# Computing v of all heads first, in 512-column matmuls over eight PSUM banks, and regrouping the projections around it

## The chip, the cores and the metric

The kernel runs on one core of a Trainium2 chip. The metric is the device time of one execution in microseconds, median of three runs. The core has a matrix engine (TensorE, PE in the profile), a vector engine (VectorE, DVE), an activation engine (ScalarE, ACT), GpSimd (POOL), SyncE (SP, which here issues most of the DMAs), and 16 DMA engines. Instructions of one engine are executed in the order in which they are queued; engines wait for each other by semaphores.

## The reference

One layer of a bidirectional encoder over 512 positions and 2048 features, all in float32:

```python
h = _rmsnorm(x, attn_norm_w[l])
proj = jnp.einsum('bsd,de->bse', h, w_in[l])
q_pre, fz_f, fz_b, i_pre, gate, b_gate, c_gate, h_conv = jnp.split(proj, SPLIT_OFFSETS, axis=-1)
y_rec = _hgrn2_mixer(q_pre, fz_f, fz_b, i_pre, gate, lbs_f[l], lbs_b[l], hgrn_norm_w[l])
y_conv = _short_conv_mixer(b_gate, c_gate, h_conv, conv_w[l])
mixed = jnp.concatenate([y_rec, y_conv], axis=-1)
x = x + jnp.einsum('bse,ed->bsd', mixed, w_out[l])
h2 = _rmsnorm(x, ffn_norm_w[l])
g, u = jnp.split(jnp.einsum('bsd,df->bsf', h2, w_gate_up[l]), 2, axis=-1)
x = x + jnp.einsum('bsf,fd->bsd', jax.nn.silu(g) * u, w_down[l])
return _rmsnorm(x, final_norm_w)
```

Each of the eight pieces of `proj` has 1024 features, which is 8 heads (or 8 convolution groups) of 128. `i_pre` is v of the recurrence, unchanged; q goes through silu; the forward and backward f give decays and keys. `_hgrn2_mixer` runs, for each head, a gated linear recurrence over the positions in both directions and a norm over the head's 128 features.

## The kernel before

**Arithmetic.** Every float32 operand is split into two parts of a faster format, hi (a cast on ACT, L143 or L959) and lo = x - hi (a subtraction on DVE, L133). A product of two such operands is three matmuls, hi x hi, hi x lo, lo x hi: `mm3`, L185 to L187. `gemm` makes one row block of a projection (128 features x 512 positions) from 16 blocks of 128 input features: 48 matmuls of 512 columns.

**Units.** Two row blocks of the projection that share the input are also computed as a `Unit` of seven products (a 2 x 2 scheme of Strassen's kind). The operand combinations of the activations, the "forms", are made once in `start`: `b11`, `b12`, `b21`, `b22` and the derived `t1` to `t4`. A product is 16 matmuls, eight of 512 columns (L1027) and eight of 256 (L1029). Sums and splits of the weights for each product are made on DVE and ACT just ahead of it, and DVE adds up the results.

**Stages around the change.**
- `start` loads the input x block by block (`kt`, 16 blocks), splits it, and computes v of head pairs 0 and 1 while the blocks arrive: for each block 8 outputs of 128 positions x 256 features, one `mm3` each, in eight banks. Then it makes three projections of head 0 (q, f forward, f backward) by `gemm`. The norm factor of the input is made inside the first two: `rstd_steps` sums the squares by small matmuls (L213), copies the sums and takes mean + eps on DVE (L218, L221), the power -1/2 on POOL (L224), multiplies it into a diagonal on DVE (L230), and spreads it over the partitions by a matmul (L235). The result is `R` (as a row) and `rk` (as a column).
- `stream` runs 15 units: q of heads 1 to 4, then convolution and gate rows. Two generators are stepped between products: `rest`, with what `start` left to do, and `later`, with silu and convolution steps. Results go to DRAM (`qd`, `gd`, `md`, `zd`, `vd`).
- `heads` runs the recurrence of the eight heads, one after the other. The recurrence of a head is nine dependent levels, each a few small matmuls (L262, L273, L280, L288, L316) with several DVE operations between, and a norm (L213 to L235 again). So that TensorE has work meanwhile, projections of later heads are put between: `windows` lists for each period what is computed in it, `size` counts it in segments of one `mm3`, and the recurrence's 15 steps are spread evenly over the segments (`PARTS`, `segment`). In these windows lie v of pairs 2 and 3 (`values_mm`, with 256-column matmuls, 384 in all), q of heads 5 to 7, f of heads 1 to 7, and convolution rows.
- `out_proj` and `ffn` follow.

The order on TensorE, DVE and ACT is the order in which the program is written (`manual_schedule`) in `start`, `stream`, `heads` up to its first yield, and `ffn`; later in `heads` that of TensorE alone.

Of the kernel before, what the change touches and what calls it, by code (L numbers as in the profile page):

```python
# [358 lines left out]
def start(k, xT, wi, wp, vd, zd):  # L359
# [9 lines left out]
    order = [j + 4 * i for i in (0, 2, 1, 3) for j in range(4)]  # L369

    def forms(j, xa, xb):
# [10 lines left out]
        for i, (name, src) in enumerate((("t1", b11), ("t2", b22), ("t4", b21))):  # L382
            f = k.slot(F32R, k.sp if 3 * j + i < 5 else k.hp)
            nc.scalar.copy(f[:, :H], src)
            F[name, j] = f[:, :H], f[:, H:], vap(f, 0, [[H, 2], [1, H]])
            todo.append((f[:, H:], src, f[:, :H].bitcast(F32)))
# [16 lines left out]
    for n, kt in enumerate(order):
# [8 lines left out]
        if kt % 2 == 0:  # L412
            j = kt // 2
            s = slice((j % 4) * T, (j % 4 + 1) * T)
            e = slice((j % 2) * T, (j % 2 + 1) * T)
            for i in range(2):
                nc.sync.dma_start(out=raw[i][j // 4][:, s], in_=wi[i, j // 4, :, s])
        if kt % 4 == 0:
            w = [[k.wp.tile([P, QW], F32R, tag=t, name=k.nm(t), bufs=HLB) for t in ("hi", "lo")]
                 for _ in range(2)]  # L420
# [21 lines left out]
    ws = k.weights(wp[0])  # L442
    held = []
    for i in range(2):
        for t in range(4):
            if t % 2 == 0:
                v = k.slot()
            h = v[:, (t % 2) * 256:(t % 2 + 1) * 256]
            if t % 2:
                nc.vector.tensor_copy(out=h, in_=pss[i][t][:, :256])  # L450
            else:
                nc.scalar.copy(h, pss[i][t][:, :256])
            held.append(h)
    act = [(kt, hT[kt]) for kt in range(KT)]
    rs = k.rstd_steps(k.ssum, DM, keep=k.xsum)

    def t3(j, x):
        h, l = [a[:, H:].bitcast(F32) for a in hT[j + 8][:2]]
        nc.vector.scalar_tensor_tensor(out=x, in0=x, scalar=col(C_ATT + j), in1=h,
                                       op0=ALU.mult, op1=ALU.subtract)  # L460
        k.sub(x, l, x)

    def rows():
        rc, pb = next(rs)
        nc.scalar.copy(k.R, pb)
        nc.vector.tensor_copy(out=k.rk, in_=rc)
        for n, h in enumerate(held):
            nc.scalar.activation(h, h, AF.Copy, scale=k.rk[:, n % 4:n % 4 + 1])
            nc.sync.dma_start(out=vd[n], in_=h)
# [8 lines left out]
    for i in range(3):
        ticks = [lambda: work(WORK2)] * KT
        if i == 0:  # L480
            ticks[10] = lambda: next(rs)
        if i == 1:
            ticks[2] = rows
            ticks[5] = lambda: store(0)
        if i < 2:
            ticks[3] = lambda: ws.extend(k.weights(wp[i + 1]))
        else:
            b12 = load_b12(k, xT)
            ticks[2] = lambda: store(1)
            for j in range(8):  # L490
                ticks[8 + j] = lambda j=j: t3(j, b12[j])
        zs.append(k.gemm([ws.pop(0) for _ in range(2)], act, tick=lambda: ticks.pop(0)()))
    for j in range(8):
        for name, kt, c in (("b11", j, lo), ("b21", j + 8, lo), ("b22", j + 8, hi), ("t3", j, hi)):
            F[name, j] = *[a[:, c] for a in hT[kt][:2]], hT[kt][2][:, :, c]

    def rest():
        while later:
# [4 lines left out]
        for j in range(8):
            h, l, _ = F["t3", j]
            nc.scalar.copy(h, b12[j])
            k.sub(l, b12[j], h.bitcast(F32))
            yield
# [110 lines left out]
def heads(k, ctx, hT, w0, z0, wi, wp, gd, qd, vd, md):  # L618
# [26 lines left out]
    def values_mm(w):  # L645

        two = [k.bank("g") for _ in range(2)]
        outs = [two[t // 2][:, (t % 2) * 256:(t % 2 + 1) * 256] for t in range(4)]
        for i, (kt, t) in enumerate((kt, t) for t in range(4) for kt in range(KT)):
            hi, lo = w[kt // 4]  # L650
            e = slice((kt % 4) * 256, (kt % 4 + 1) * 256)
            s = slice(t * P, (t + 1) * P)
            k.mm3(outs[t], hT[kt][0][:, s], hT[kt][1][:, s], hi[:, e], lo[:, e],
                  kt == 0, kt == KT - 1)
            if i % 2:
                segment()
        return outs

    def values(srcs):
        vs = []  # L660
        for t, src in enumerate(srcs):
# [869 lines left out]
```

## Time and profile before

| | us |
|---|---|
| median of 3 runs | 2321.79 (2321.28 to 2322.09) |
| the profiled execution | 2326.49 |
| its span in the trace | 2324.7 |
| TensorE busy | 2284.5 (98%) |
| VectorE busy | 1869.2 (80%) |
| ScalarE busy | 1126.2 (48%) |
| GpSimd busy | 222.7 (10%) |

A busy TensorE is not one at its peak: its matmuls are pipelined, and their ends overlap the starts of the next. What a matmul costs is therefore read from the distance of two starts. Idle time is printed in square brackets behind the instruction that came after it, with what released it. The page follows the chain of work that ended last to TensorE for 74% of the span. The granted clock of TensorE is a share of full speed; the chip has two levels, 1.2 and 2.4 GHz.

### The profile page before, as it was taken

The numbers are of one execution on the slowest core, as the hardware profiler recorded it, in microseconds if no ns is written. First come the engines' busy times: TensorE is split into PE (matmuls) and PEld (weight loads), VectorE is DVE, ScalarE is ACT, GpSimd is POOL, SyncE is SP. The second block draws the span as 40 slices with busy tenths as digits, with TensorE's granted clock in tenths as the row PEclk, the third lists the DMA queues.
The fourth block names the chain that finished last, engine by engine and source line by source line (L and its number), as shares of the span: only waits on it lengthen the run. The fifth ranks groups of instructions, "written<-read, shape, count | busy, mean of one in ns | idle before, by whom it ended". The sixth has DMA issues, their size and how long they took to land.

```text
span 2324.7 us, 34542 instructions
## 1 busy us (share of the span) xinstructions
PE 2284.5 (98%) x13138; PEld 2000.1 (86%) x13138; DVE 1869.2 (80%) x2605; ACT 1126.2 (48%) x1597; POOL 222.7 (10%) x254
## 2 busy tenths in 40 slices
PE   8999999999999999999999999999999989999997
PEld 8888888788887888888888888888888888888997
DVE  8889878766666765679888888888889988788877
ACT  7555545333333343345555555555555544444453
POOL 0031100000000000001111111111110001111110
PEclk9999999999999999999999999999999999999998
DMA  6377766222122265588888888889898686896974
GB/s 237 128 210 208 200 187 226 73 81 88 68 78 82 99 203 183 198 259 221 234 225 232 221 237 231 243 232 244 229 243 234 219 266 156 294 267 159 300 210 134
DMA packets 147525, 455.42 MB, mean 196 GB/s; under 512 B 15776, under 2 KB 39072, under 8 KB 122272
## 3 DMA queue, kind: packets, MB, share of 16 engines
q1 hardware_dynamic: 110528, 349.09, 43.7%
q0 software_dynamic: 34512, 101.99, 22.8%
q8 instruction: 103, 1.69, 0.3%
q10 hardware_dynamic: 2320, 2.15, 0.3%
q14 instruction: 62, 0.51, 0.1%
HBM read 291.75 MB, written 71.50 MB: 156 GB/s over the span
## 4 chain that ended last, share of the span: by engine, by line
PE 74%; DVE 3%; DMA 2%; issue 1%; ACT 1%; POOL 0%; POOLq 0%; SPq 0%; ACTq 0%; DVEq 0%
PE g L1027 21%; PE g L1029 11%; PE r L1027 9%; PE g L185 7%; PE g L186 7%; PE g L187 7%; PE r L1029 4%; PE r L273 2%; DVE lo L133 1%; PE r L316 1%; DMA raw<-wd 1%; DMA raw<-raw 1%; DVE d L136 1%; PE r L288 1%; DVE raw L136 1%
## 5 line engine op out<-in xcount | busy, mean ns | idle before, releaser
L133 DVE TENSOR_TENSOR lo<-raw,hi 128x1024 fp32r<-128x1024 f32 (+2 forms) x689 | 809.4, 1186 | 195.3 <-ACT hi L959 107.9
L959 ACT CAST hi<-raw 128x1024 fp32r<-128x1024 f32 (+1 forms) x581 | 598.1, 1031 | 635.7 <-PE g L1027 243.3
L1027 PE MATMUL g<-s,hi 128*128 128x512 f32 x2560 | 895.3, 391 | 2.2 <-ACT d L1045 2.2
L1029 PE MATMUL g<-s,lo 128*128 128x256 f32 x2560 | 719.2, 281 | 1.9 <-DVE lo L133 1.9
L1027 PEld LDWEIGHTS g<-s,hi 128*128 128x128 f32 x2560 | 479.8, 187 | 107.7 <-ACT d L1045 2.9
L1029 PEld LDWEIGHTS g<-s,lo 128*128 128x128 f32 x2560 | 483.6, 189 | 2.2 <-DVE lo L133 2.2
L1027 PE MATMUL r<-s,hi 128*128 128x512 f32 x1048 | 370.0, 392 | 2.1 <-DVE d L136 1.1
L1029 PE MATMUL r<-s,lo 128*128 128x256 f32 x1048 | 293.6, 280 | 0.0
L930 POOL DMA_DIRECT2D raw<-raw x175 | 152.2, 877 | 1207.6 <-DVE s L133 284.7
L1027 PEld LDWEIGHTS r<-s,hi 128*128 128x128 f32 x1048 | 196.1, 187 | 46.7 <-ACT s L1299 1.3
L1029 PEld LDWEIGHTS r<-s,lo 128*128 128x128 f32 x1048 | 198.0, 189 | 0.2 <-issue 0.2
L185 PE MATMUL g<-s,hi 128*128 128x256 f32 (+1 forms) x576 | 192.5, 334 | 2.6 <-ACT s L1130 2.6
L187 PE MATMUL g<-s,lo 128*128 128x256 f32 (+1 forms) x576 | 192.1, 334 | 2.1 <-DVE lo L133 2.1
L186 PE MATMUL g<-s,hi 128*128 128x256 f32 (+1 forms) x576 | 192.4, 334 | 0.0
L143 ACT CAST hi<-raw 128x1024 fp32r<-128x1024 f32 (+1 forms) x108 | 105.1, 984 | 161.6 <-PE g L186 149.9
L185 PE MATMUL g<-x,hi 128*128 128x512 f32 x416 | 176.8, 425 | 0.0
L136 DVE TENSOR_TENSOR d<-d 128x512 f32<-128x512 f32 x219 | 151.6, 692 | 27.3 <-ACT d L1051 20.7
L187 PE MATMUL g<-x,lo 128*128 128x512 f32 x416 | 163.0, 392 | 0.0
L186 PE MATMUL g<-x,hi 128*128 128x512 f32 x416 | 162.8, 391 | 0.0
L1027 PE MATMUL g<-x,hi 128*128 128x512 f32 x360 | 128.0, 396 | 2.6 <-ACT d L1043 2.6
L136 DVE TENSOR_TENSOR d<-d,r 128x512 f32<-128x512 f32 x146 | 100.3, 687 | 33.3 <-PE r L1029 30.7
L185 PEld LDWEIGHTS g<-s,hi 128*128 128x128 f32 x576 | 110.3, 191 | 14.1 <-ACT s L1130 2.8
(188 smaller groups left out, 3125.8 us busy)
## 6 DMA issues: line engine op xcount, KB each, us to landing
raw<-wg SPq DMA_DIRECT2D x88, 1024.0 KB, 5.5
raw<-raw POOLq DMA_DIRECT2D x161, 512.0 KB, 9.0
raw<-wp SPq DMA_DIRECT2D x56, 1024.0 KB, 4.9
hfd<-s SPq DMA_DIRECT2D x130, 256.0 KB, 7.9
s<-hfd SPq DMA_DIRECT2D x130, 256.0 KB, 5.6
raw<-wd SPq DMA_DIRECT2D x32, 1024.0 KB, 7.3
raw<-wo SPq DMA_DIRECT2D x16, 1024.0 KB, 5.3
raw<-wd SPq DMA_DIRECT2D x16, 768.0 KB, 5.0
```

The lines of the kernel that those rows point to most:

```text
L133: self.nc.vector.tensor_tensor(out=out, in0=a, in1=b, op=ALU.subtract)
L136: self.nc.vector.tensor_tensor(out=out, in0=a, in1=b, op=ALU.add)
L143: self.nc.scalar.copy(hi, src)
L185: mm(out, ahi, bhi, start=start, stop=False, **kw)
L186: mm(out, ahi, blo, start=False, stop=False, **kw)
L187: mm(out, alo, bhi, start=False, stop=stop, **kw)
L273: nc.tensor.matmul(ps[:, g * P:(g + 1) * P], kc[:, g * P:(g + 1) * P], vap(Qt, g * P, dims), start=True, stop=True)
L288: nc.tensor.matmul(ps[:, j * 256:(j + 1) * 256], Kt[:, d, s * P:(s + 1) * P], Qt[:, 1 - d, tq:tq + 256], start=True, stop=True)
L930: self.k.nc.gpsimd.dma_start(out=out, in_=a, accum_op=ALU.add)
L959: k.nc.scalar.copy(hi, src)
L1027: mm(vap(ps, 0, [[H, 2], [1, H]]), w[0][:, s], f, start=start and j == 0, stop=False, skip_group_check=True)
L1029: mm(ps[:, H:], w[1][:, s], bh, start=False, stop=stop and j == self.nj - 1, skip_group_check=True)
```

## The change

- `start` computes v of all eight heads. Its weights are laid out anew, 128 x 1024 for each of 16 input blocks, and each of the eight outputs is a whole bank of 128 positions x 512 features, in matmuls of 512 columns. The last two input blocks are taken bank by bank, and each bank is copied out and stored to `vd` as it is done, not yet scaled by `rk`.
- Head 0's three projections are no longer made in `start`. q of heads 0 to 5 come from three units, f forward and backward of head 0 from one more, so `stream` has 17 units (`QS = 6`).
- The rstd steps move into the generator `rest`, and `t3` is made with the other forms.
- `heads` loads v from DRAM and scales it on ACT (16 operations); `values_mm` and q of head 5 are gone from its windows, and the windows are dealt anew.

```diff
-QS = 4
+QS = 6
...
-        vd = k.dp.tile([8, P, 256], F32, name="vd")
+        vd = k.dp.tile([8, P, T], F32, name="vd")
...
+        stt(out=b12, in0=b22, scalar=w, in1=b12, op0=ALU.mult, op1=ALU.subtract)
...
-        for i, (name, src) in enumerate((("t1", b11), ("t2", b22), ("t4", b21))):
+        for i, (name, src) in enumerate((("t1", b11), ("t2", b22), ("t4", b21), ("t3", b12))):
...
+    def products(n, outs):
+        kt = order[n]
+        for i, t in outs:
+            s, e = slice(t * P, (t + 1) * P), slice(i * T, (i + 1) * T)
+            k.mm3(pss[i][t], hT[kt][0][:, s], hT[kt][1][:, s], ws[n][0][:, e], ws[n][1][:, e],
+                  n == 0, n == KT - 1)
+
+    outs = [(i, t) for i in (1, 0) for t in (3, 2, 1, 0)]
...
-        e = slice((kt % 4) * 256, (kt % 4 + 1) * 256)
-        for i in range(2):
-            for t in range(4):
-                s = slice(t * P, (t + 1) * P)
-                k.mm3(pss[i][t][:, :256], hT[kt][0][:, s], hT[kt][1][:, s], w[i][0][:, e],
-                      w[i][1][:, e], n == 0, n == KT - 1)
+        if n < KT - 2:
+            products(n, outs)
...
+    for m, (i, t) in enumerate(outs):
+        for n in (KT - 2, KT - 1):
+            products(n, [(i, t)])
+        v = k.slot()
+        if m % 2:
+            nc.vector.tensor_copy(out=v, in_=pss[i][t])
         else:
-            b12 = load_b12(k, xT)
-            ticks[2] = lambda: store(1)
-            for j in range(8):
-                ticks[8 + j] = lambda j=j: t3(j, b12[j])
-        zs.append(k.gemm([ws.pop(0) for _ in range(2)], act, tick=lambda: ticks.pop(0)()))
+            nc.scalar.copy(v, pss[i][t])
+        nc.sync.dma_start(out=vd[4 * i + t], in_=v)
+        work(WORK)
...
     def rest():
         while later:
             work(1)
             yield
-        store(2)
-        yield
-        for j in range(8):
-            h, l, _ = F["t3", j]
-            nc.scalar.copy(h, b12[j])
-            k.sub(l, b12[j], h.bitcast(F32))
-            yield
+        rs = k.rstd_steps(k.ssum, DM, keep=k.xsum)
+        next(rs)
+        yield
+        yield
+        yield
+        rc, pb = next(rs)
+        nc.scalar.copy(k.R, pb)
+        nc.vector.tensor_copy(out=k.rk, in_=rc)
...
-    for h in range(1, QS, 2):
+    for h in range(0, QS, 2):
         unit([3 * h, 3 * h + 3], lambda i, z, h=h: later.append(silu(z, qd[h + i])))
+    unit([1, 2], lambda i, z: nc.sync.dma_start(out=zd[i], in_=z))
...
+        V[i] = []
+        c = slice(i % 2 * 256, (i % 2 + 1) * 256)
+        for t in range(4):
+            v = k.rp.tile([P, 256], F32, tag="v", name=k.nm("v"), bufs=8)
+            nc.sync.dma_start(out=v, in_=vd[i // 2 * 4 + t, :, c])
+            nc.scalar.activation(v, v, AF.Copy, scale=rk[:, t:t + 1])
+            V[i].append(v)
...
                [(q, 1), (v, 0), (c, 0), (fb, 1)],
-               [(q, 2), (v, 1), (q, 5), (fb, 2)],
-               [(q, 3), (v, 2), (fb, 3)],
-               [(q, 4), (q, 6), (fb, 4)],
-               [(v, 3), (fb, 5)],
-               [(q, 7), (fb, 6)],
-               [(c, 1), (fb, 7)],
-               [(c, 2), (c, 3), (c, 4)],
+               [(q, 2), (v, 1), (q, 6), (fb, 2)],
+               [(q, 3), (c, 1), (fb, 3)],
+               [(q, 4), (v, 2), (q, 7), (fb, 4)],
+               [(q, 5), (fb, 5)],
+               [(v, 3), (c, 2), (fb, 6)],
+               [(fb, 7)],
+               [(c, 3), (c, 4)],
                [(c, 5)]]
```

What the diff does not show is the order that comes of it. On TensorE, around the first L235 (the names are out<-in; `g` and `r` are banks, `m` the small bank, `x` activations, `s_866` the diagonal), before:

```order
L187 MATMUL g_886<-x_125,lo_806 128x512
L185 MATMUL g_886<-x_159,hi_805 128x512
L186 MATMUL g_886<-x_159,hi_805 128x512
L187 MATMUL g_886<-x_159,lo_806 128x512
L185 MATMUL g_886<-x_192,hi_805 128x512
L186 MATMUL g_886<-x_192,hi_805 128x512
L187 MATMUL g_886<-x_192,lo_806 128x512
L235 MATMUL m_896<-s_866,ones 128x512
L185 MATMUL g_886<-x_228,hi_805 128x512
L186 MATMUL g_886<-x_228,hi_805 128x512
L187 MATMUL g_886<-x_228,lo_806 128x512
L185 MATMUL g_886<-x_427,hi_805 128x512
```

After (L975 and L977 are the lines L1027 and L1029 of before):

```order
L975 MATMUL g_904<-x_486,hi_872 128x512
L977 MATMUL g_904<-x_486,lo_874 128x256
L975 MATMUL g_904<-x_529,hi_872 128x512
L977 MATMUL g_904<-x_529,lo_874 128x256
L975 MATMUL g_904<-x_576,hi_872 128x512
L977 MATMUL g_904<-x_576,lo_874 128x256
L235 MATMUL m_927<-s_902,ones 128x512
L975 MATMUL r_931<-x_267,hi_876 128x512
L977 MATMUL r_931<-x_267,lo_878 128x256
```

L235 stood inside the second projection, 24 matmuls behind L213; it now stands between the first and the second product of the first unit, 16 matmuls behind L213, which directly follows the last matmul of v.

On VectorE, around the operations of the same rstd (L218, L221 and L230), before:

```order
L133 TENSOR_TENSOR d_506<-d_506 128x256
L378 SCALAR_TENSOR_TENSOR d_675<-d_675,neg,d_506 128x256
L379 SCALAR_TENSOR_TENSOR d_675<-d_675,sm 128x256
L218 COPY xsum<-m_856 128x4
L221 TENSOR_SCALAR ms_861<-m_856 128x4
L230 TENSOR_TENSOR s_866<-ident,rc_864 128x512
L133 TENSOR_TENSOR s_847<-d_506,s_847 128x256
L133 TENSOR_TENSOR s_849<-d_675,s_849 128x256
```

After:

```order
L456 COPY s_861<-g_105 128x512
L133 TENSOR_TENSOR lo_874<-raw_864,hi_872 128x1024
L133 TENSOR_TENSOR lo_878<-raw_864,hi_876 128x1024
L136 TENSOR_TENSOR raw_866<-raw_866 128x1024
L133 TENSOR_TENSOR raw_864<-raw_864,raw_866 128x1024
L133 TENSOR_TENSOR lo_884<-raw_866,hi_880 128x1024
L133 TENSOR_TENSOR lo_888<-raw_866,hi_886 128x1024
L218 COPY xsum<-m_892 128x4
L221 TENSOR_SCALAR ms_897<-m_892 128x4
L230 TENSOR_TENSOR s_902<-ident,rc_900 128x512
```

The three stood among operations on the forms. They now stand behind the copy of the last bank of v and six operations of 128x1024 that prepare the weights of the first unit.

On TensorE in the recurrence of head 6, from L262 to the second L273, before:

```order
L262 MATMUL m_6262<-ones,s_6228 128x1 x4
L273 MATMUL r_6268<-Q_6226,s_6231 128x128 x4
L185 MATMUL g_6213<-x_472,hi_6205 128x512
L186 MATMUL g_6213<-x_472,hi_6205 128x512
L187 MATMUL g_6213<-x_472,lo_6206 128x512
L185 MATMUL g_6213<-x_510,hi_6205 128x512
L186 MATMUL g_6213<-x_510,hi_6205 128x512
L187 MATMUL g_6213<-x_510,lo_6206 128x512
L185 MATMUL g_6213<-x_554,hi_6205 128x512
L186 MATMUL g_6213<-x_554,hi_6205 128x512
L187 MATMUL g_6213<-x_554,lo_6206 128x512
L273 MATMUL r_6290<-Q_6226,s_6274 128x128 x4
```

After:

```order
L262 MATMUL m_6067<-ones,s_6042 128x1 x4
L273 MATMUL r_6073<-Q_6040,s_6045 128x128 x4
L185 MATMUL g_6030<-x_155,hi_6022 128x512
L186 MATMUL g_6030<-x_155,hi_6022 128x512
L187 MATMUL g_6030<-x_155,lo_6023 128x512
L185 MATMUL g_6030<-x_192,hi_6022 128x512
L186 MATMUL g_6030<-x_192,hi_6022 128x512
L187 MATMUL g_6030<-x_192,lo_6023 128x512
L273 MATMUL r_6092<-Q_6040,s_6079 128x128 x4
```

Nine matmuls stood between the first two L273, now six. Over the whole row of L262 in the program, the matmuls of L185 to L187 from each L262 to the next were 108 of 512 columns in the first period and 144 in the sixth and seventh; they are 108, 144, 144, 132, 108, 132 and 96 now, and six between steps in the first, fifth, seventh and eighth period. Of these, 39 stood behind L235 in all of the periods named of before, and 39, 39, 39, 27, 39, 27 and 27 stand there now.

## Rows read from the trace of the kernel before

**Rows 1.** The page's first section: busy us, share of the span, instructions; TensorE.

```profile
PE 2284.5 (98%) x13138; PEld 2000.1 (86%) x13138; DVE 1869.2 (80%) x2605; ACT 1126.2 (48%) x1597; POOL 222.7 (10%) x254
```

**Rows 2.** Timeline of TensorE in `start`: start, duration, line, operation, [idle <-releaser].

```profile
5.92 0.58 PE L185 MATMUL g<-hi,x 128*128 128x256 f32 x1 [5.92 <-ACT hi L143]
...
12.06 0.28 PE L186 MATMUL g<-lo,x 128*128 128x256 f32 x1
12.18 0.28 PE L187 MATMUL g<-hi,x 128*128 128x256 f32 x1
...
55.13 0.40 PE L185 MATMUL g<-x,hi 128*128 128x512 f32 x1
55.36 0.40 PE L186 MATMUL g<-x,hi 128*128 128x512 f32 x1
55.59 0.39 PE L187 MATMUL g<-x,lo 128*128 128x512 f32 x1
...
89.65 0.39 PE L1027 MATMUL g<-x,hi 128*128 128x512 f32 x1
```

**Rows 3.** Timeline of TensorE: first matmul of a product and of the next.

```profile
317.62 0.39 PE L1027 MATMUL g<-x,hi 128*128 128x512 f32 x1
...
320.40 0.39 PE L1027 MATMUL r<-x,hi 128*128 128x512 f32 x1
```

**Rows 4.** Groups by line and shape, TensorE, 405.76 to 840: v of pairs 2, 3.

```profile
L185 PE MATMUL g<-hi,x 128*128 128x256 f32 x128 | 37.7, 295 | 0.0
```

**Rows 5.** Timeline of TensorE, VectorE and GpSimd: the rstd of the input.

```profile
62.63 0.95 PE L213 MATMUL m<-ones,s 128*128 128x1 f32 x8
...
69.03 1.02 PE L235 MATMUL m<-s,ones 128*128 128x512 f32 x2
...
58.99 1.22 DVE L133 TENSOR_TENSOR lo<-raw,hi 128x1024 fp32r<-128x1024 f32 x1
60.13 0.42 DVE L133 TENSOR_TENSOR d<-d 128x256 f32<-128x256 f32 x1
...
64.14 0.15 DVE L221 TENSOR_SCALAR ms<-m 128x4 f32<-128x4 f32 x1
65.43 0.69 DVE L230 TENSOR_TENSOR s<-ident,rc 128x512 f32<-128x512 f32 x1 [1.13 <-POOL rc L224]
```

**Rows 6.** Timeline of TensorE, then a stretch: busy by engine, PEclk, DMA share, GB/s.

```profile
342.60 0.50 PE L1027 MATMUL g<-x,hi 128*128 128x512 f32 x1 [2.58 <-ACT d L1043]
...
344.00:346.00 2.00, 2.00 (x8) 1.64 (x7) 2.00 (x3) 1.41 (x2) 0.90 (x1) 0.50 0.66 226
```

**Rows 7.** The same at the first recurrence matmul.

```profile
405.76 0.27 PE L262 MATMUL m<-ones,s 128*128 128x1 f32 x1 [1.63 <-DVE s L139]
...
408.00:410.00 2.00, 2.00 (x7) 1.61 (x6) 1.70 (x4) 0.00 (x0) 0.00 (x0) 0.50 0.32 85
410.00:412.00 2.00, 2.00 (x11) 1.81 (x11) 0.89 (x2) 0.62 (x1) 0.00 (x0) 0.66 0.12 46
```

**Rows 8.** Stretches of two periods: us, busy PE, PEld, DVE, ACT, POOL; TensorE's waits.

```profile
405.76:450.22 44.46, 42.67 (x206) 34.05 (x207) 33.39 (x63) 15.19 (x22) 1.04 (x1) 0.96 0.18 62
668.29:716.92 48.63, 48.61 (x243) 39.79 (x242) 34.61 (x63) 16.88 (x24) 1.01 (x1) 1.00 0.21 76
...
PE m L235 <- DVE s L230: 0.7, 1, 0.7
PE r L280 <- DVE Q L139: 0.6, 1, 0.6
PE r L288 <- DVE Q L139: 0.5, 1, 0.5
```

**Rows 9.** Timeline of TensorE and VectorE from L235 to the next head's first products.

```profile
440.41 1.10 PE L235 MATMUL m<-s,ones 128*128 128x512 f32 x2 [0.72 <-DVE s L230]
...
446.61 0.69 DVE L139 TENSOR_TENSOR T<-T 128x512 f32<-128x512 f32 x1
447.22 0.69 DVE L139 TENSOR_TENSOR s<-s,s 128x512 f32<-128x512 f32 x1
```

More of the change, by code (lines that the diff above doesn't have):

```diff
@@ L356, in body, with start @@
             ffn(k, forms, fd, rho, wg, wd, hfd, x1d, out)
-def start(k, xT, wi, wp, vd, zd):
+def start(k, xT, wi, vd):
     nc = k.nc
@@ L381, in forms @@
         todo = []
-        for i, (name, src) in enumerate((("t1", b11), ("t2", b22), ("t4", b21))):
[L383 to L386, printed above, removed]
+        for i, (name, src) in enumerate((("t1", b11), ("t2", b22), ("t4", b21), ("t3", b12))):
+            if name == "t3":
+                h, l, f = *[a[:, hi] for a in hT[j][:2]], hT[j][2][:, :, hi]
+            else:
+                f = k.slot(F32R, k.sp if 3 * j + i < 5 else k.hp)
+                h, l, f = f[:, :H], f[:, H:], vap(f, 0, [[H, 2], [1, H]])
+            nc.scalar.copy(h, src)
+            F[name, j] = h, l, f
+            todo.append((l, src, h.bitcast(F32)))
         yield
@@ L411, in start @@
         nc.sync.dma_start(out=x, in_=xT[kt])
[L412 to L415, printed above, removed]
-            for i in range(2):
[L417 to L420, printed above, removed]
+        if n % 2 == 0:
+            raw = k.wp.tile([P, DM], F32, tag="raw", name=k.nm("raw"), bufs=RAWB)
+        src = raw[:, (n % 2) * QW:(n % 2 + 1) * QW]
+        for i in (1, 0) if n == 0 else (None,):
+            c = slice(0, QW) if i is None else slice(i * T, (i + 1) * T)
+            nc.sync.dma_start(out=src[:, c], in_=wi[kt, :, c])
         t = k.xp.tile([P, 2, T], F32R, tag="x", name=k.nm("x"))
@@ L423, in start @@
         k.split_scaled(t[:, 0], t[:, 1], x, col(C_ATT + kt))
-        if kt % 2 == 0:
-            for i in range(2):
-                k.split(w[i][0][:, e], w[i][1][:, e], raw[i][j // 4][:, s])
+        ws[n] = [k.wp.tile([P, QW], F32R, tag=t, name=k.nm(t), bufs=HLB) for t in ("hi", "lo")]
+        for i in (1, 0) if n == 0 else (None,):
+            c = slice(0, QW) if i is None else slice(i * T, (i + 1) * T)
+            k.split(ws[n][0][:, c], ws[n][1][:, c], src[:, c])
         sq = k.slot() if n else k.ssum
@@ L441, in start @@
     k.add(k.ssum, k.ssum, before)
[L442 to L469, printed above, removed]
@@ L493, in start @@
     for j in range(8):
[L494 removed]
+        for name, kt, c in (("b11", j, lo), ("b21", j + 8, lo), ("b22", j + 8, hi)):
             F[name, j] = *[a[:, c] for a in hT[kt][:2]], hT[kt][2][:, :, c]
@@ L603, in stream @@
             zs = []
-            for n in range(3):
-                zs.append(k.slot(pool=None if n else k.sp))
+            for n in range(2):
+                zs.append(k.slot())
                 nc.sync.dma_start(out=zs[n], in_=zd[n])
@@ L615, in stream, with heads @@
     return ws, zs
-def heads(k, ctx, hT, w0, z0, wi, wp, gd, qd, vd, md):
+def heads(k, ctx, hT, w0, z0, wp, gd, qd, vd, md):
     nc = k.nc
@@ L643, in segment @@
             extra.pop(0)
[L645 to L661, printed above, removed]
-            v = k.rp.tile([P, 256], F32, tag="v", name=k.nm("v"), bufs=8)
-            nc.scalar.activation(v, src, AF.Copy, scale=rk[:, t:t + 1])
-            vs.append(v)
-        return vs
     def proj_mm(i):
@@ L728, in v @@
     def v(i):
-        if i < 2:
-            V[i] = []
-            for t in range(4):
-                V[i].append(k.rp.tile([P, 256], F32, tag="v", name=k.nm("v"), bufs=8))
-                nc.sync.dma_start(out=V[i][t], in_=vd[4 * i + t])
-        else:
-            V[i] = values(values_mm([x for j in range(2) for x in k.weights(wi[i, j])]))
+        V[i] = []
[5 more added lines that the diff above has]
+            V[i].append(v)
     Q, C = {}, {}
     def q(h):
-        if 1 <= h <= QS:
+        if h < QS:
             z = Q[h] = k.slot(pool=k.sp)
```

41 lines of the change are left out of this document (12 added, 29 removed).

## The prediction

> **What bounds the kernel now.** I read the page's engine table first: TensorE is busy 98% of the span [rows 1], so what the change does to the time is the change in TensorE's own work plus the change in its few waits. Next I read its timeline at the start. Matmuls of 256 columns start 0.120 us apart, those of 512 columns 0.227 us; the part that computes v lasts from 5.92 to 55.13, the three projections of head 0 behind it until 89.65 [rows 2]. Then the stream: a product of 16 matmuls takes 2.78 us (317.62 to 320.40), so a unit of seven takes 19.4 us [rows 3]. Then the places where TensorE waits or is about to: the rstd of the input [rows 5], the two waits that were followed by half clock [rows 6, 7], and the head periods with few matmuls between recurrence steps [rows 8, 9].
>
> The profiled execution lasted 2326.49 us (span 2324.7), 4.70 us above the median 2321.79. The terms below are differences taken from it; I add them to the median.
>
> **The change, part by part: TensorE's own work.**
> - v at the start. 384 matmuls of 256 columns become 384 of 512. Before, 384 x 0.120 = 46.1 us of the 49.2 us between 5.92 and 55.13 [rows 2]; the other 3.1 us are the first loads and half clock, which I keep. After: 384 x 0.2266 + 3.1 = 90.1 us. **+40.9.** The wider weight loads (768 KB for each of 16 blocks against 5.45 us of matmuls) are slower than the rate at which they are used only under 145 GB/s; I cost them at nothing, with TensorE's 87 us as cover.
> - Head 0's three projections leave: 144 x 0.2266 [rows 2]. **-32.6.** q of head 5 leaves the windows: 48 x 0.2266, **-10.9.** v of head pairs 2 and 3 leaves them: 384 matmuls of 256 columns (three lines of 128 each, one shown) x 0.120 [rows 2, 4], **-46.1.**
> - These four rows and two that shared units otherwise come as two more units: 2 x 19.4 [rows 3], **+38.8.**
>
> Sum of work: **-9.9 us**. It is small because two matmuls of 256 cost 0.240 us where one of 512 costs 0.227 [rows 2]. The Trainium skill's page "TensorE: Matmul & The Clock Gate", section "Wait — 56ns, not 53.3ns?", speaks against even that: it gives N / 2.4 GHz + about 2.5 ns from start to start, 109 and 216 ns, by which all of v would save 768 x 0.1092 - 384 x 0.2158 = 1.0 us and not the 5.2 us of my rows. By the page the total below would be 4.2 us higher; the trace's 0.120 disagrees with the page, and I go by the trace.
>
> **The new wait behind v.** Before, the rstd chain was hidden: its first matmuls (L213) stood at 62.63, the one that needs the result (L235) at 69.03, with 24 matmuls of a projection between [rows 5]. Now L213 stands directly behind the last v matmul and L235 after one product, and the DVE queue is in another order: copy of the last bank, six operations of 128x1024 for the first unit's weights, and only then the copy of the sums, ms, and the diagonal that L235 reads. Let T0 be the end of the v matmuls. The last copy starts at T0 + 0.4 at the earliest (a matmul lasts about 0.4 from start, [rows 2]); copy 0.6, six times 1.14 (58.99 to 60.13), the sums 0.2, ms to diagonal by way of POOL 1.29 (64.14 to 65.43), diagonal 0.69 [rows 5]: L235 can start at T0 + 10.0. TensorE has for these 10 us only L213 (0.9) and the product (2.78): it idles 6.3 us. DVE also has the forms of the last blocks to make ahead of the last copy, eight operations for each of two blocks where two groups of v last 2.7 us; that puts it 0.4 to 1.9 us late, I take 1.2. Then the clock: a wait of 2.58 us was followed by 0.50 of full clock [rows 6], and one of 1.63 us by 0.50 and 0.66 over two stretches of 2 us, which cost (1 - 0.50) x 2 + (1 - 0.66) x 2 = 1.7 us [rows 7]. The new wait is longer than both. 6.3 + 1.2 + 1.7: **+9.2**, bounds 8.0 (no delay but the clock) and 10.7 (the delay at 1.9 and 0.8 more of clock). Behind L235 nothing on TensorE waits anew: the splits of the next three products are finished while it waits.
>
> **Stream to heads.** Before, the first recurrence matmul (L262) waits 1.63 us for DVE, and 1.7 us of clock follow [rows 7]: 3.3 us. In the new order DVE makes head 0's gates and the powers of T before the last evacuations, since q0, f0 and b0 no longer come last. Behind the last bank that TensorE delivers, DVE has six operations of 0.6 and one split of 1.14 [rows 5, 9], 4.8 to 5.4 us, against 27 matmuls, 6.1 us. The wait goes: **-3.3**, bounds 0 (the evacuations are late, the wait stays) and -3.3. That the L1027 wait of 2.58 us before 342.60 comes again I cost at nothing; what it depends on is unchanged.
>
> **The windows of the heads.** The work that left was the filling between the steps of the recurrence. Three head periods, the fifth, seventh and eighth, now have 6 matmuls between two steps where the densest before had 9 or 12. One such period existed: the first, 405.76 to 450.22 [rows 8]. A period with 144 filling matmuls lasts 48.63 us, so its other work is 48.63 - 144 x 0.2266 = 16.0. The first has 108: 108 x 0.2266 + 16.0 = 40.5, and lasted 44.46. Of the 4.0 lost, 1.7 are the clock after its entry, 2.3 are waits for DVE inside (L235 0.7, L280 0.6, L288 0.5 are named) [rows 8]. The 144 period has none. So 2.3 for each of the three new ones. Further, where the period before leaves only 27 matmuls between L235 and the next L262 (into the fifth, seventh and eighth), DVE's chain from L235 at 440.41 to its last product, which ends about 447.9, takes 7.5 us [rows 9] against 0.53 + 27 x 0.2266 = 6.65: a wait of 0.85. 3 x (2.3 + 0.85): **+9.5**. Bounds: 5 (the entries wait for nothing, and half of one period's waits fall away because its weights are split elsewhere) and 13 (two of the waits are long enough for the clock, 2 x 1.7). The scaling of v by ACT (16 small operations) and the DMAs of v stand beside 40 us of TensorE work in a period where ACT is busy 15 of 44 us [rows 8]: nothing, and 1 us if an o copy behind them is late.
>
> **Sum:** -9.9 + 9.2 - 3.3 + 9.5 = +5.5: 2321.79 + 5.5 = 2327.3, taken as 2327.
>
> **The rivals.**
> - *The thin windows cost nothing.* The three periods hide their DVE work as the 144 periods do: the term falls from 9.5 to about 1, and the time is 2321.79 - 9.9 + 9.2 - 3.3 + 1 = 2318.8. For it: DVE is busy only 33.4 of 44.5 us in the first period. Against it: that same period waited at three named places [rows 8]. This is "the same". With the wait behind v at its lower bound too (8.0) and nothing lost in the periods, 2316.6: the side opposite to my forecast. It decides at the point where the three periods together lose under 0.5 us.
> - *The clock falls in the thin windows.* One wait of 1.6 us or more in each, as at 405.76 [rows 7], adds 3 x 1.7: 2332.4. For it: two waits that stand close (L280, L288). Against: 0.5 to 0.7 each was not followed by it in the first period.
> - *The wait at the start of the heads stays.* Some other operation of DVE is last instead: term 0, 2330.6. For it: DVE's queue there is as long as before; against: 27 matmuls now cover the last evacuation.
> - *Width brings nothing.* A matmul of 512 in the eight-bank order takes two of 256, 0.240: 384 x 0.0134 = 5.1 more, 2332.4. The projections' 0.227 speaks against it [rows 2].
>
> **How the numbers follow.** Anything within 0.2% (4.6 us) counts as no change, about what a measurement of this kernel can tell. My forecast, 2322 to 2330: 0.45, of which 0.27 lies above 2326.4. Thin windows free: 0.22 in "same", 0.09 faster. Clock in the windows 0.11, heads' wait stays 0.10, width 0.03: all slower. So faster 0.09, same 0.18 + 0.22 = 0.40, slower 0.27 + 0.24 = 0.51. The range 2318 to 2335 leaves out the fast case and a sum of two slow ones.
>
> **What would show it.** In the new profile: v's last matmul at about 96; then TensorE idle some 7 us before L235, released by DVE's diagonal, and a granted clock of one half behind it; the first unit's end about 9 us later than 2.78 us a product would give. No idle before the first L262. Waits for DVE of 0.5 to 1 us at L262, L280, L288 and L235 in the fifth, seventh and eighth period, which last 44 and not 40 us, and none in the others. I am wrong if L235 waits under 5 us, if those three periods show no idle, or if the first L262 still waits over 1 us.

## The result: the changed kernel is 0.5% slower, 2334.22 us against 2321.94

| | before | after |
|---|---|---|
| median, us | 2321.94 (2321.28 to 2323.11, 4 runs) | 2334.22 (2332.87 to 2334.89, 4 runs) |
| ratio to before, 95% interval | | 1.0054 (1.0042 to 1.0066) |
| the profiled execution, us | 2326.49 | 2334.89 |
| its span, us | 2324.7 | 2332.9 |

The time lies inside the range of the prediction and on the side that was forecast, 7 us above the likeliest value and 0.8 us below the upper end. TensorE is busy for the same share of a longer span. From the page of the changed kernel, the line that answers to [rows 1]:

```profile
PE 2281.3 (98%) x12786; PEld 1977.3 (85%) x12786; DVE 1880.8 (81%) x2610; ACT 1137.2 (49%) x1604; POOL 226.0 (10%) x260
```

TensorE was busy 3 us less and the span is 8 us longer: the change took work away and put waits in its place.

**Where v ends and the stream begins.** Timeline of TensorE in the changed kernel (start, duration, line, operation, [idle before <- releaser]); the answer to [rows 2, 5]:

```profile
95.75 0.39 PE L187 MATMUL g<-hi,x 128*128 128x512 f32 x1
95.98 0.95 PE L213 MATMUL m<-ones,s 128*128 128x1 f32 x8
97.57 0.49 PE L975 MATMUL g<-x,hi 128*128 128x512 f32 x1 [0.65 <-ACT hi L907]
99.08 0.38 PE L977 MATMUL g<-x,lo 128*128 128x256 f32 x1 [1.01 <-DVE lo L133]
...
101.61 0.28 PE L977 MATMUL g<-x,lo 128*128 128x256 f32 x1
106.93 2.05 PE L235 MATMUL m<-s,ones 128*128 128x512 f32 x2 [5.04 <-DVE s L230]
```

Timeline of VectorE in the same stretch:

```profile
96.60 1.28 DVE L456 COPY s<-g 128x512 f32<-128x512 f32 x2
97.80 2.35 DVE L133 TENSOR_TENSOR lo<-raw,hi 128x1024 fp32r<-128x1024 f32 x2
100.07 1.22 DVE L136 TENSOR_TENSOR raw<-raw 128x1024 f32<-128x1024 f32 x1
101.33 1.23 DVE L133 TENSOR_TENSOR raw<-raw,raw 128x1024 f32<-128x1024 f32 x1
102.47 2.36 DVE L133 TENSOR_TENSOR lo<-raw,hi 128x1024 fp32r<-128x1024 f32 x2
104.74 0.16 DVE L218 COPY xsum<-m 128x4 f32<-128x4 f32 x1
...
106.09 0.69 DVE L230 TENSOR_TENSOR s<-ident,rc 128x512 f32<-128x512 f32 x1 [1.13 <-POOL rc L224]
```

The reader sees the queue of VectorE being worked off: two copies of banks, six operations on weights, and the sums of squares only at 104.74, though TensorE had them ready at 97. L235 starts 10.95 us after the v matmuls end. The granted clock is the third number from the end of a stretch's row; in the two stretches behind the wait it is half (each stretch: us, busy PE, PEld, DVE, ACT, POOL, PEclk, DMA share, GB/s):

```profile
107.00:109.00 2.00, 2.00 (x3) 0.97 (x4) 2.00 (x3) 0.00 (x0) 0.00 (x0) 0.50 0.00 0
109.00:111.00 2.00, 2.00 (x7) 1.69 (x7) 1.26 (x2) 0.59 (x1) 0.00 (x0) 0.53 0.00 0
```

The second unit starts at 126.43 (timeline of TensorE):

```profile
126.43 0.39 PE L975 MATMUL g<-x,hi 128*128 128x512 f32 x1
```

From 95.98 to there are 30.45 us. L213 (0.94), L235 (0.46) and seven products of 2.78 us [rows 3] account for 20.86 of them, so the stretch is 9.6 us longer than its work. Of these, 8.6 are the listed waits (0.65 + 1.01 + 5.04) and the clock (0.50 and 0.47 of 2 us lost); the other 1.0 lies in gaps that are not listed.

**The periods of the heads.** A period runs from the L262 that opens one head's recurrence, its entry, to the next head's. The answer to [rows 8]: the first, fifth, seventh and eighth period of the changed kernel (the last one up to the last L235 of the heads), and TensorE's largest waits in all eight (total us, times, longest):

```profile
459.40:502.71 43.31, 41.40 (x208) 32.71 (x207) 32.83 (x60) 15.54 (x23) 1.03 (x1) 1.00 0.24 86
647.62:692.98 45.36, 43.01 (x206) 34.08 (x207) 31.73 (x61) 15.19 (x22) 1.01 (x1) 0.96 0.17 59
740.05:783.11 43.06, 40.43 (x195) 31.55 (x195) 30.25 (x58) 13.82 (x21) 1.01 (x1) 0.96 0.17 62
783.11:838.06 54.95, 53.27 (x262) 42.81 (x263) 39.93 (x73) 20.87 (x32) 9.94 (x16) 1.00 0.41 139
```

```profile
PE m L235 <- DVE s L230: 2.9, 4, 0.7
PE r L273 <- DVE Q L139: 2.8, 6, 0.5
PE m L262 <- DVE s L139: 2.5, 3, 1.2
PE r L288 <- DVE Q L139: 1.5, 3, 0.5
PE r L280 <- DVE Q L139: 1.1, 2, 0.6
```

Before, only the first of these periods had waits. The three new ones were entered with a wait, and behind the two longer of these waits they ran at half clock (timeline, then stretches):

```profile
647.62 1.05 PE L262 MATMUL m<-ones,s 128*128 128x1 f32 x8 [1.22 <-DVE s L139]
...
740.05 1.05 PE L262 MATMUL m<-ones,s 128*128 128x1 f32 x8 [0.99 <-DVE s L139]
...
783.11 1.05 PE L262 MATMUL m<-ones,s 128*128 128x1 f32 x8 [0.27 <-DVE s L139]
```

```profile
650.00:652.00 2.00, 2.00 (x7) 1.58 (x6) 1.87 (x4) 0.00 (x0) 0.00 (x0) 0.55 0.00 0
652.00:654.00 2.00, 2.00 (x11) 1.91 (x10) 0.44 (x2) 0.62 (x1) 0.00 (x0) 0.60 0.00 0
...
741.00:743.00 2.00, 2.00 (x11) 1.90 (x12) 1.13 (x3) 0.42 (x1) 0.00 (x0) 0.84 0.00 0
743.00:745.00 2.00, 2.00 (x6) 1.51 (x6) 1.86 (x4) 0.44 (x1) 0.00 (x0) 0.50 0.00 0
745.00:747.00 2.00, 2.00 (x13) 1.87 (x12) 0.57 (x2) 0.18 (x1) 0.00 (x0) 0.81 0.00 0
```

**The two traces laid side by side.** The first L262 starts at 405.76 before and 459.40 after: +53.6. TensorE work that came forward is 47 us of it, and the wait behind v with its clock 9.6. Gone are the 1.6 of idle time at the L262, some 0.5 around the first L235 of before, and 0.8 late in the stream. There the wait of [rows 6] came again, at 2.52 us, but the half clock behind it did not, 1.7 us less; the next wait grew from 0.58 to 1.12. Timeline of the changed kernel, then the stretch behind:

```profile
398.69 0.50 PE L975 MATMUL g<-x,hi 128*128 128x512 f32 x1 [2.52 <-ACT d L991]
...
400.00:402.00 2.00, 2.00 (x14) 1.72 (x13) 2.00 (x4) 1.75 (x4) 0.88 (x1) 1.00 0.86 273
```

From the first L262 to the last L235 of the heads it is 420.85 before and 378.66 after: -42.2. Behind that the program is the same, and the changed kernel's execution was 3.3 us the shorter: in the last stage a cast waited for a weight DMA in both, but TensorE waited 2.60 us behind it before and 0.90 after, and half clock (0.50 in 2276 to 2278) followed only before. Timeline of TensorE, first before, then after:

```profile
2274.18 0.39 PE L185 MATMUL g<-s,hi 128*128 128x256 f32 x1 [2.60 <-ACT s L1130]
```

```profile
2283.99 0.39 PE L185 MATMUL g<-s,hi 128*128 128x256 f32 x1 [0.90 <-ACT s L1078]
```

The spans differ by 8.2 us and the medians by 12.3; without this last place the traces say 53.6 - 42.2 = +11.4. Whether the other executions of the kernel before go without the wait at 2274 no trace shows.

### The profile page after: what moved, and what is told of

Same layout as the page of the kernel before. It is cut to its first block, busy times and chain, and to the rows that moved or that the text cites. A ratio compares the mean times of both kernels' runs of the same rounds, so it can differ in the third digit from the quotient of the medians.

```text
span 2332.9 us, 33911 instructions
## 1 busy us (share of the span) xinstructions
PE 2281.3 (98%) x12786; PEld 1977.3 (85%) x12786; DVE 1880.8 (81%) x2610; ACT 1137.2 (49%) x1604; POOL 226.0 (10%) x260
## 4 chain that ended last, share of the span: by engine, by line
PE 68%; DVE 5%; DMA 3%; issue 2%; ACT 1%; POOL 0%; POOLq 0%; ACTq 0%; DVEq 0%; SPq 0%
PE g L975 22%; PE g L977 11%; PE r L975 8%; PE g L185 6%; PE g L186 6%; PE g L187 5%; PE r L977 4%; PE r L273 2%; DMA raw<-raw 2%; DVE lo L133 1%; PE r L316 1%; DVE raw L136 1%; PE r L288 1%; ACT hi L907 1%; DVE d L136 0%
## 5 line engine op out<-in xcount | busy, mean ns | idle before, releaser
L975 PE MATMUL g<-s,hi 128*128 128x512 f32 x2592 | 906.5, 391 | 2.2 <-ACT d L993 2.2
L977 PE MATMUL g<-s,lo 128*128 128x256 f32 x2592 | 728.1, 281 | 1.0 <-DVE lo L133 1.0
L975 PEld LDWEIGHTS g<-s,hi 128*128 128x128 f32 x2592 | 485.8, 187 | 109.1 <-ACT d L993 2.9
L977 PEld LDWEIGHTS g<-s,lo 128*128 128x128 f32 x2592 | 489.7, 189 | 1.4 <-DVE lo L133 1.3
L975 PE MATMUL r<-s,hi 128*128 128x512 f32 x1064 | 375.7, 392 | 2.3 <-DVE d L136 1.3
L977 PE MATMUL r<-s,lo 128*128 128x256 f32 x1064 | 298.1, 280 | 0.0
L878 POOL DMA_DIRECT2D raw<-raw x181 | 157.1, 876 | 1214.8 <-DVE s L133 286.7
L975 PEld LDWEIGHTS r<-s,hi 128*128 128x128 f32 x1064 | 199.1, 187 | 47.6 <-issue 1.6
L977 PEld LDWEIGHTS r<-s,lo 128*128 128x128 f32 x1064 | 201.1, 189 | 0.2 <-issue 0.2
L187 PE MATMUL g<-s,lo 128*128 128x256 f32 (+1 forms) x576 | 191.5, 333 | 2.0 <-DVE lo L133 2.0
L185 PE MATMUL g<-s,hi 128*128 128x256 f32 (+1 forms) x576 | 191.8, 333 | 0.9 <-ACT s L1078 0.9
L185 PE MATMUL g<-x,hi 128*128 128x512 f32 x352 | 153.2, 435 | 0.0
L975 PE MATMUL g<-x,hi 128*128 128x512 f32 x408 | 143.6, 393 | 3.2 <-ACT d L991 2.5
L187 PE MATMUL g<-x,lo 128*128 128x512 f32 x352 | 138.7, 394 | 0.0
L186 PE MATMUL g<-x,hi 128*128 128x512 f32 x352 | 138.3, 393 | 0.0
L187 PEld LDWEIGHTS g<-s,lo 128*128 128x128 f32 x576 | 109.7, 190 | 13.5 <-DVE lo L133 2.2
```

Source lines behind the costliest of these rows:

```text
L185: mm(out, ahi, bhi, start=start, stop=False, **kw)
L186: mm(out, ahi, blo, start=False, stop=False, **kw)
L187: mm(out, alo, bhi, start=False, stop=stop, **kw)
L878: self.k.nc.gpsimd.dma_start(out=out, in_=a, accum_op=ALU.add)
L975: mm(vap(ps, 0, [[H, 2], [1, H]]), w[0][:, s], f, start=start and j == 0, stop=False, skip_group_check=True)
L977: mm(ps[:, H:], w[1][:, s], bh, start=False, stop=stop and j == self.nj - 1, skip_group_check=True)
```

## The experiments

Two theories stood against each other: that the 12 us are two separate groups of waits that can be taken away where they arise (the norm's chain queued behind weight work, and recurrence periods with too few matmuls), or that VectorE is simply late over the whole stretch, so that a wait removed comes back at the next place. Ratios are to the kernel before, run on the same chip in the same session; a difference of 0.001 is 2.3 us. The changed kernel stands at 1.0054 (1.0042 to 1.0066), so a difference between two of these ratios is known to about 0.0015, 3.5 us; where the text goes finer than that, it goes by the traces.

| | what | ratio (95%) | median, us | before, us |
|---|---|---|---|---|
| e1 | L235 behind two more products | 1.0019 (1.0010 to 1.0028) | 2327.08 | 2323.30 |
| e2 | full windows but the last | 1.0018 (1.0009 to 1.0027) | 2326.25 | 2323.30 |
| e3 | both | 0.9984 (0.9974 to 0.9993) | 2319.64 | 2323.30 |
| e4 | entries of the thin periods covered | 1.0029 (1.0017 to 1.0041) | 2329.20 | 2323.30 |
| e5 | v in halves of 256 | 1.0065 (1.0052 to 1.0077) | 2338.37 | 2322.69 |
| e6 | e3, entry of the eighth covered | 0.9993 (0.9984 to 1.0002) | 2321.47 | 2322.69 |
| e7 | e3, all periods full | 0.9973 (0.9961 to 0.9984) | 2316.21 | 2322.69 |

**e1: the norm's matmul later.**

```diff
         next(rs)
         yield
         yield
         yield
+        yield
+        yield
+        yield
+        yield
         rc, pb = next(rs)
```

> The changed kernel with one edit: the generator of the norm yields four times more before it issues L235, which so stands behind the third product of the first unit and not behind the first. Theory (TensorE waits there only for the diagonal that VectorE makes too late): the diagonal comes at the same time as before, about 11 us after the last v matmul, and TensorE now has two more products, 5.6 us, to do by then. The wait of 5.04 us at 106.93 is gone, and with it the 1.9 us of half clock behind it (0.50 and 0.53 to 0.94 of 2 us stretches): 7.0 us faster than the changed kernel, near 2327. Rival (VectorE is the bound of that stretch, and TensorE only meets it elsewhere): the second or third product waits for its lo instead, and the gain is under 2 us, 2332 or more.

Measured: 0.0035 less than the changed kernel, 8.1 us; in the trace the first L262 starts 7.3 us earlier, at 452.12. L235 now follows its predecessor without a wait, and the clock stays full (timeline of TensorE, then the stretch around it):

```profile
106.90 0.28 PE L981 MATMUL r<-s,lo 128*128 128x256 f32 x1
107.02 1.02 PE L235 MATMUL m<-s,ones 128*128 128x512 f32 x2
```

```profile
106.00:108.00 2.00, 2.00 (x11) 1.40 (x10) 2.00 (x3) 0.00 (x0) 0.00 (x0) 1.00 0.00 0
```

VectorE began the diagonal at 105.83, 10.12 us after the v matmuls, against 10.11 in the changed kernel: as late as ever. TensorE had two more products to do. The second and third product waited for nothing. What stayed are the waits of 0.65 and 1.00 us at the first product. The rival falls.

**e2: the windows filled.**

```diff
-QS = 6
+QS = 4
...
-               [(q, 4), (v, 2), (q, 7), (fb, 4)],
+               [(q, 4), (v, 2), (fb, 4)],
                [(q, 5), (fb, 5)],
                [(v, 3), (c, 2), (fb, 6)],
-               [(fb, 7)],
+               [(q, 7), (fb, 7)],
```

> The changed kernel with QS = 4: q of heads 4 and 5 are no longer a unit in the stream but two projections in the windows, and q of head 7 moves to the last window of a head, so that the fifth and seventh period have 48 segments instead of 32; only the eighth stays at 32. Work: two projections of 48 matmuls, 21.8 us, for a unit of 19.4, so 2.4 us more. Theory (the thin periods cost what the trace shows beyond their matmuls: 1.4 + 4.9 + 1.2 + 5.3 us in the fourth to seventh, waits and half clock): that goes, 12.8 us, less 2.4: 10.4 faster than the changed kernel, near 2324. Rival (the loss is in VectorE's total work over the heads and only moves to other periods): the periods of 48 segments now show waits, and the time is 2.4 us longer than the changed kernel's or the same, 2334 to 2337.

Measured: 0.0036 less than the changed kernel, 8.4 us, although TensorE has 2.4 us more to do. The fourth to seventh period last 48.64, 48.64, 48.64 and 47.06 us; the first three are what 144 filling matmuls cost without any wait (48.63 in [rows 8]), and no wait is listed in them. The seventh has 132 and ends with the wait at the entry of the eighth, which is still thin: 0.99 us before L262 at 774.51, and behind it the clock that the changed kernel did not lose at this place:

```profile
776.00:778.00 2.00, 2.00 (x9) 1.80 (x9) 1.03 (x4) 0.00 (x0) 0.00 (x0) 0.51 0.00 0
```

The eighth period lasts 56.31 us for it, against 54.95, and its entry wait is 0.99 for 0.27: together the 2 us by which the gain is short of the 10.4 expected. The waits for VectorE did not move to the periods that were filled: the rival falls here too.

**e3: both.**

> Both edits, the norm later and the full windows. Theory: the two places are independent, and the gains add up: 17.4 us faster than the changed kernel, near 2317, which is 5 us faster than the kernel before. Rival (either gain is given back later): at or above the kernel before, 2322 or more.

Measured: 0.0070 less than the changed kernel, 16 us, and 3.7 us faster than the kernel before, by an interval that excludes no change. The two gains, 8.1 and 8.4, add up within their intervals, as two independent places would; the rival falls.

**e4: only the entry of the thin periods.** A lead is the number of segments (one `mm3` each) that a window puts ahead of the first step of the recurrence; the steps are spread over the rest.

```diff
-        count[:] = 0, sum(size[f] for f, i in window if (f, i) not in stored), LEAD if n == 1 else LEADS
+        count[:] = 0, sum(size[f] for f, i in window if (f, i) not in stored), LEAD if n == 1 else 4 if n in (5, 7) else LEADS
```

> The changed kernel with a lead of 4 segments in the fifth and seventh window: 36 instead of 27 matmuls stand between L235 of the period before and the L262 that opens the thin one, and 3 instead of 9 and 3 instead of 6 in two gaps inside the thin period. All work is the same. Theory (the half clock of 1.7 us in each thin period follows the wait at its entry, 1.22 and 0.99 us): without the entry wait the clock stays full; gain 1.22 + 0.99 + 2 x 1.7 = 5.6 us, less what the two thinner gaps lose, at most 2 x 9 matmuls of 0.227 = 4.1: 1.5 to 5.6 us faster than the changed kernel, and the granted clock of the two periods is 1.00. Rival (the clock falls because the period is thin, whatever its entry): the entry waits go, the clock still falls to one half inside the two periods, and the time is within 2 us of the changed kernel's or above it.

Measured: 0.0025 less, 5.8 us, at the upper end; in the trace the fourth to seventh period together last 178.66 us instead of 182.78, 4.1 less. The entry waits are gone, and so is the half clock behind them: 1.00 in every stretch of the first 6 us of both periods, and in the whole of the seventh (a stretch of the fifth, then the seventh):

```profile
650.00:652.00 2.00, 2.00 (x14) 1.81 (x13) 1.74 (x4) 0.23 (x1) 0.00 (x0) 1.00 0.80 311
...
738.40:778.06 39.66, 36.98 (x186) 28.52 (x184) 29.51 (x58) 14.47 (x21) 1.01 (x1) 1.00 0.19 67
```

But the wait at L235 grew from 0.75 to 1.4 in both, since 3 matmuls stand between L213 and L235 there instead of 6, and behind one of the two, in the fifth period, the clock fell, against the expectation (timeline, then a stretch behind each):

```profile
679.06 1.38 PE L235 MATMUL m<-s,ones 128*128 128x512 f32 x2 [1.42 <-DVE s L230]
...
770.68 1.10 PE L235 MATMUL m<-s,ones 128*128 128x512 f32 x2 [1.43 <-DVE s L230]
```

```profile
681.00:683.00 2.00, 2.00 (x6) 1.52 (x5) 1.87 (x4) 1.02 (x2) 0.00 (x0) 0.50 0.10 38
...
772.00:774.00 2.00, 2.00 (x11) 1.61 (x10) 1.87 (x4) 0.67 (x2) 0.00 (x0) 1.00 0.00 0
```

So a thin period does not lower the clock by itself; the falls seen follow a wait, and not every wait has one. In e1 and e5, whose entries are those of the changed kernel (1.19 and 0.99 us in e1, 1.21 and 0.99 in e5), the clock fell behind both again.

**e5: is width worth anything?**

```diff
-            k.mm3(pss[i][t], hT[kt][0][:, s], hT[kt][1][:, s], ws[n][0][:, e], ws[n][1][:, e],
-                  n == 0, n == KT - 1)
...
+            for c in range(2):
+                d = slice(i * T + c * 256, i * T + (c + 1) * 256)
+                k.mm3(pss[i][t][:, c * 256:(c + 1) * 256], hT[kt][0][:, s], hT[kt][1][:, s],
+                      ws[n][0][:, d], ws[n][1][:, d], n == 0 and c == 0, n == KT - 1 and c == 1,
+                      skip_group_check=True)
```

> The changed kernel with every 512-column matmul of v taken as two of 256, on the two halves of the same bank: 768 instead of 384 matmuls, the same order otherwise. By the starts in the trace of the kernel before (0.120 and 0.2266 us): 768 x 0.120 - 384 x 0.2266 = 92.2 - 87.0 = 5.1 us longer than the changed kernel, about 2339. Rival, the rule of the Trainium skill's page on TensorE by which two matmuls of 256 cost 218 ns and one of 512 216: 1.0 us longer, about 2335.

Measured: 0.0011 more than the changed kernel, 2.6 us, between the two expectations and by ratios whose intervals overlap; the traces separate them. Stretches from 20 us to the end of v, e5 first, then the changed kernel:

```profile
20.00:99.69 79.69, 79.69 (x667) 79.69 (x666) 51.94 (x98) 37.56 (x73) 0.00 (x0) 1.00 0.39 144
```

```profile
20.00:95.98 75.98, 75.98 (x336) 62.89 (x336) 52.19 (x98) 37.98 (x72) 0.00 (x0) 1.00 0.41 149
```

79.69 / 667 = 0.1195 us for a matmul of 256 columns and 75.98 / 336 = 0.2261 for one of 512: 768 x 0.1195 - 384 x 0.2261 = 4.9 us for all of v, against an estimate of 1.0 by the rule of the Trainium skill's page "TensorE: Matmul & The Clock Gate", section "Wait — 56ns, not 53.3ns?" (109 and 216 ns). The measurement decides. The whole of v, from its first matmul, lasted 94.28 against 90.36, 3.9 more; in e5 the matmuls left the slower rate of the first microseconds earlier, at 9.2 instead of 11.8, which gave it about the other 1. The row also suggests why: with 256 columns the weight load (PEld) is busy for the whole stretch, 79.69 of 79.69; with 512 it is not, 62.89 of 75.98. That is read, not tested.

**e6 and e7: the eighth period.** e6 gives e3 a lead of 4 in the eighth window; e7 sets `QS = 2` in e3, deals one q to each window, and fills the eighth with four convolution rows:

```diff
+               [(q, 2), (v, 1), (fb, 2)],
+               [(q, 3), (fb, 3)],
+               [(q, 4), (v, 2), (fb, 4)],
+               [(q, 5), (fb, 5)],
+               [(v, 3), (q, 6), (fb, 6)],
+               [(q, 7), (fb, 7)],
+               [(c, 1), (c, 2), (c, 3), (c, 4)],
```

> The kernel of e3 (norm later, full windows) with a lead of 4 segments in the eighth period's window: 36 matmuls instead of 27 cover the entry, two gaps inside lose 6 and 3. In e3 that entry waited 0.99 us, and half clock followed. Theory: both go, 0.99 + 1.7, less at most 2.0 for the thinner gaps: 0.7 to 2.7 us faster than e3, near 2318. Rival (the wait only moves to the thinner gaps): the same as e3 within 1 us.

> The kernel of e3 with QS = 2: q of heads 2 and 3 too are projections in their windows (one unit, 19.4 us, for two projections, 21.8: 2.4 us more), and four convolution rows fill the eighth period to 64 segments; every period from the second on has 48 or more. Theory (thin periods cost waits and clock): the eighth period's losses go, 2.5 us inside, 0.99 at the entry and 1.7 of clock, 5.2 in all, less 2.4: 2.8 us faster than e3, near 2317. Rival: the eighth period's waits are covered anyway or come back elsewhere, and the time is e3's plus 2.4, near 2322.

e6 shows no gain; its ratio is 0.0009 above e3's, inside the intervals. Its entry wait is gone, but the waits in the gaps inside grew (L273 from 0.53 to 0.72, a new one of 0.56 at L288), that at L235 from 0.75 to 1.40, and the clock fell there (timeline, stretch):

```profile
800.58 1.99 PE L235 MATMUL m<-s,ones 128*128 128x512 f32 x2 [1.40 <-DVE s L230]
```

```profile
802.00:804.00 2.00, 2.00 (x5) 1.34 (x4) 1.36 (x3) 0.00 (x0) 0.54 (x1) 0.50 0.33 133
```

And there was less to win than both expectations say: the half clock behind this entry was seen in e2. In e3's profiled execution the same wait was not followed by it (timeline, the stretch behind it):

```profile
767.35 1.05 PE L262 MATMUL m<-ones,s 128*128 128x1 f32 x8 [0.99 <-DVE s L139]
```

```profile
769.00:771.00 2.00, 2.00 (x11) 1.78 (x11) 1.27 (x4) 0.00 (x0) 0.00 (x0) 1.00 0.00 0
```

e7 is 0.0011 below e3. That is the 2.8 us expected, but the two intervals overlap, so that it beats e3 is not shown; its rival, 2322, lies outside its interval. It is 0.27% (0.16 to 0.39) below the kernel before, 2316.21 us. Its eighth period has no idle at all:

```profile
752.89:820.97 68.08, 68.08 (x333) 55.88 (x331) 46.20 (x76) 23.48 (x35) 9.92 (x16) 1.00 0.39 136
```

It also agrees with the account. The prediction's saving of 9.9 us of TensorE work, with 2 x 2.4 given back for the two units, another 2.8 gained at the start of the heads (below), and 1.7 of waits left at the first product: -9.9 + 4.8 - 2.8 + 1.7 = -6.2 us; measured -6.3 by ratio (-3.7 to -9.1).

## Why the prediction was right, and where it was 7 us short

- **TensorE's work, -9.9.** Right in its parts: v lasted 5.62 to 95.98, 90.4 us, for 90.1; 0.2261 a matmul for 0.2266. e7, which has the saving without the waits, is faster by about what is left of it.
- **The wait behind v, +9.2.** Right in place, cause and size: 9.6 by the start of the second unit, of which 6.7 are listed waits and 1.9 clock; L235 came at 10.95 us after v for 11.2 (10.0 and 1.2 of delay). e1 gave 8.1 back by moving one matmul.
- **The start of the heads, -3.3.** Right in mechanism: no idle before the first L262 at 459.40, and a granted clock of 1.00 in the first period. But that period lasts 43.31 instead of 44.46, 1.15 less and not the 1.7 of the clock, since the waits inside it grew: 1.63 + 1.15 = 2.8.
- **The windows, +9.5.** Right in mechanism and in the three periods; this is the term that was mis-sized. Take a period at its matmuls x 0.2266 + 16.0 (the eighth: 17.1, which is what it took before beyond its 192 matmuls): the fourth to eighth lasted 1.4, 4.9, 1.2, 5.3 and 2.5 us longer, **15.2** in sum, above the term's own upper bound of 13. (A period ends with the wait at the next entry, which is most of the 1.4 and 1.2.) The entries were priced at 3 x 0.85 = 2.55 and took 1.22 + 0.99 + 0.27 = 2.5. Inside, 3 x 2.3 = 6.9 were expected; the listed waits are 6.4 (at L273, which the prediction did not name, as well as at L280, L288 and L235), and the 2.9 that remain are put down to gaps too short to be listed. The clock was priced at nothing and took 1.7 in the fifth and 1.7 in the seventh period. So of the 5.7 us missing 3.4 are the clock and 2.4 are short gaps.
- **The step that failed** is the price of the clock in the windows. The sum put it at nothing, because a fall was held to need a wait of 1.6 us; it came behind 1.22 and 0.99, in two of the three periods, and took 3.4 us. The prediction had it as a rival, at 3 x 1.7, 2332.4 and a chance of 0.11; its likeliest case should have held part of it, since the entry waits of 0.85 were in the sum, and that they are harmless rested on waits of 0.5 to 0.7. With the short gaps the forecast becomes 2327.3 + 3.4 + 2.4 = 2333.1, against 2334.22. That the time stayed inside the range with one term beyond its own bound owes something to luck.
- **The other rivals.** The thin windows did cost something, the wait at the heads did not stay, and width brought what its rows said (e5).

As they came, the terms are -9.9 + 9.6 - 2.8 + 15.2 = 12.1. The two traces, with 0.8 less late in the stream, say 11.4, and the medians 12.3.

## What to carry to other kernels

Before moving work out of a latency-bound loop, count it as cover: 432 matmuls left the recurrence, 10 us were saved on TensorE, and 15 us came back as waits for dependent VectorE steps and as clock; giving two projections back cost 2.4 us and returned nearly 11 (e2). What a second pair returned (e7) lies inside the intervals. When a stage that hid a chain of small operations is removed, look where the chain's operations stand in each engine's queue: here one matmul moved behind two products was worth 8 us, with VectorE as late as before.

## What the runs showed of the hardware beyond what was expected

- Half clock came behind waits shorter than the 1.6 us seen before, and not behind every wait of a given length: 0.99 us was followed by it at 740.05 in the changed kernel and at 774.51 in e2, and not at 767.35 in e3; 1.42 us was at 679.06 in e4, and 1.43 at 770.68 in the same execution was not. Each of these falls cost about 1.7 us. In this kernel a short wait in front of small matmuls is therefore a chance of 1.7 us more, not a fixed price; what decides it these runs leave open.
- Longer waits were no surer. The wait late in the stream ([rows 6] and its like) stands in all nine traces: 2.58 us before, 2.77 in e2, 2.56 in e5 and 2.69 in e7 were followed by half clock, and 2.52 in the changed kernel, 2.69 in e1, 2.53 in e3, 2.63 in e4 and 2.71 in e6 were not. The fall cost 1.7 us in three of them and some 3 in e5 (0.50 from 402 to 408). Two profiled executions can so differ by that much at a place that the change left alone.
- At the start of the program the matmuls of 512 columns start 0.43 us apart until 11.8 us in the changed kernel, twice the later 0.23, and those of 256 in e5 0.21 until 9.2, for 0.12 later, with the first matmuls at 5.62 and 5.41. It looks like half clock, and the prediction calls it that, but the clock column shows 1.00 there (timeline of the changed kernel, then the stretch), so the profile does not show its cause:

```profile
10.50 0.63 PE L186 MATMUL r<-lo,x 128*128 128x512 f32 x1
10.93 0.63 PE L187 MATMUL r<-hi,x 128*128 128x512 f32 x1
...
6.00:12.00 6.00, 5.92 (x14) 4.34 (x14) 3.68 (x5) 4.23 (x7) 0.00 (x0) 1.00 1.01 401
```
